# A two-layer hybrid decoder trunk: the last two weight sums of a feed-forward unit made by adding transfers instead of VectorE adds

## The chip, the cores and the metric

The kernel runs on one core of a Trainium2 chip. The metric is the device time of one execution in microseconds (us). Before the change three runs took 1273.28 us in the median, from 1272.17 to 1274.06.

Names used below: PE is TensorE (matmuls), PEld its weight loads, DVE is VectorE, ACT is ScalarE, POOL is GpSimd, SP is SyncE, which issues most DMA transfers. SBUF is the on-chip memory, PSUM holds matmul results. Every engine works through its own queue in order.

## The reference, cut to what matters

Two layers over 528 positions (16 learned meta tokens and 512 real ones) of width 1024. Each layer has a normalised input projection into two groups of heads (forgetting attention and retention), an output projection, and a SwiGLU feed-forward network (FFN) of width 2816. The change is in the FFN alone:

```python
hn = rmsnorm(h, ffn_norm_g)
ff = jax.nn.silu(jnp.einsum('bld,df->blf', hn, w_gate)) * jnp.einsum('bld,df->blf', hn, w_up)
return h + jnp.einsum('blf,fd->bld', ff, w_down)
```

All of it is float32. The outputs are the 512 real positions after a last normalisation.

## The kernel before

Activations lie transposed, 128 features on the partitions and the positions along the free axis. A weight tile has 128 partitions and 8 blocks of 128 columns (NK = 8, HB = 4 is half of them). For float32 accuracy on PE each operand is split into a high part (a cast, made on ACT) and a low part (what is left, made on DVE, or on POOL in the attention stage), and each product is three matmuls: high by high, high by low, low by high.

The FFN of a layer has 22 column tiles f. The first three (PLAIN) are multiplied plainly: one product with w_gate and one with w_up for each, through `dense_steps` (matmuls at L217). The other 19 of each layer, 38 in all, are units of the class `Unit` (matmuls at L881). A unit computes the gate and the up product of one f together by Winograd's form of Strassen's scheme: the two operands are cut into 2 by 2 blocks, and seven half-size products are made where eight would be needed. For that it wants sums of weight blocks beside the weights. With a = w_gate (tile `raw`) and b = w_up (tile `fraw`), each in a first half [0:HB] and a second half [HB:NK], the sums are:

- s[HB:NK] = the second half of w_up plus its first half (tile `Sw`). SP loads the one half, POOL issues a transfer that adds the other half from DRAM into it (L908).
- b[0:HB] = the first half of w_up plus the first half of w_gate, by such an adding transfer too (L909).
- s[0:HB] = s[HB:NK] + a[0:HB], an add on DVE (L917), in `make2`.
- a[HB:NK] = a[HB:NK] + s[0:HB], an add on DVE (L928), in `make4`.

Each unit has four weight jobs, and each job is a "make" that splits its weights into high and low: make1 (w1, from raw), make2 (w2, from Sw), make3 (w3, from fraw), make4 (w4, from the second half of raw). The head of a unit multiplies with w1 (two products, the first into PSUM bank x, the second into z), the middle with w2 (x, then y) and w3 (x), the tail with w3 (x) and w4 (y). After each of the first three products into x, ACT copies the bank into `e` (L947). Between the middle and the tail, and after the tail, stands a piece of the down projection of an earlier round (L1016).

What sets the order: the program is written as a list of steps. PE's order is that of the list. For DVE, ACT, POOL and SP a scheduler orders the instructions by its own estimate of when each can run, and the waits come from who reads and writes a tile. Buffers set how far loads run ahead: three for `raw`, two each for `fraw` and `Sw`, two for each ring of split weights. `need` makes a job and up to two after it, and a unit's loads are issued when its first job is fetched.

At the start of an FFN three things run together: the plain products, with a pair of casts on ACT (L191) and subtractions on DVE (L194) for each weight tile; the normalisation's factors (L295 to L300, from sums of squares at L331 to L340); and the sums and differences of activations that the units need (L842 to L847, tiles `S`, `th`, `tl`), in which the constant `neg`, the negated FFN norm weights, is used. The loads for the first two units are issued there too.

Of the kernel before, what the change touches and what calls it, by code (L numbers as in the profile page):

```python
# [13 lines left out]
ALU = mybir.AluOpType  # L14

D = 1024
NK = D // 128
# [3 lines left out]
DEPTH = 2  # L21
# [7 lines left out]
HB = NK // 2  # L29
# [10 lines left out]
def hybrid_kernel(ctx, tc, x_t, w_in, w_fl, w_out, w_gate, w_up, w_down, vecs, b_fg, rope, decay, mask, ident, out_t):  # L40
    nc = tc.nc
# [13 lines left out]
    vec = const.tile([128, vecs.shape[1]], F32, name="vec")  # L55
# [214 lines left out]
    def at(tag, dt=F32R, shape=(128, T), bufs=None):  # L270
        return phase["att"].tile(list(shape), dt, name=tag, tag=tag, bufs=bufs)

    def fft(tag, dt=F32R, shape=(128, T), bufs=None):
        return phase["ffn"].tile(list(shape), dt, name=tag, tag=tag, bufs=bufs)
# [79 lines left out]
    V_ATTN, V_FFN, V_FIN, V_GN = 0, 2 * NK, 4 * NK, 5 * NK  # L354
# [439 lines left out]
    def ffn(l, st, real, last):  # L794
# [73 lines left out]
        def splits(hi, lo, src):  # L868
            nc.scalar.copy(hi, src)  # L869
            nc.vector.tensor_sub(lo, src, hi.bitcast(F32))  # L870
# [17 lines left out]
        class Unit:  # L888
# [12 lines left out]
            def load(self):  # L901
                if "a" not in self.t:
                    for n, src, pool, tag, bufs in (("a", w_gate, wp, "raw", 3), ("b", w_up, phase["ffn"], "fraw", 2)):
                        self.t[n] = pool.tile([128, NK, 128], F32, name=tag, tag=tag, bufs=bufs)
                        nc.sync.dma_start(self.t[n], src[l, self.f])
                    s = self.t["s"] = fft("Sw", F32, (128, NK, 128), 2)
                    nc.sync.dma_start(s[:, HB:NK], w_up[l, self.f][:, HB:NK])
                    nc.gpsimd.dma_start(s[:, HB:NK], w_up[l, self.f][:, 0:HB], accum_op=ALU.add)  # L908
                    nc.gpsimd.dma_start(self.t["b"][:, 0:HB], w_gate[l, self.f][:, 0:HB], accum_op=ALU.add)  # L909

            def make1(self, hi, lo):
                splits(hi, lo, self.t["a"])


            def make2(self, hi, lo):
                a, s = self.t["a"], self.t["s"]
                nc.vector.tensor_add(s[:, 0:HB], s[:, HB:NK], a[:, 0:HB])  # L917
                nc.scalar.activation(hi, s, AF.Copy, scale=-1.0)
                nc.vector.scalar_tensor_tensor(lo, s, -1.0, hi.bitcast(F32), ALU.mult, ALU.subtract)

# [3 lines left out]


            def make4(self, hi, lo):
                a, s = self.t["a"], self.t["s"]
                nc.vector.tensor_add(a[:, HB:NK], a[:, HB:NK], s[:, 0:HB])  # L928
                splits(hi, lo, a[:, HB:NK])

            def bank(self, n):
                def go():
# [53 lines left out]
        def down_job(p, f0, f1):  # L986

            n = f1 - f0
            t = {}

            def load():
                if t:
                    return
                t["r"] = wp.tile([128, NK, 128], F32, name="raw", tag="raw", bufs=3)
                for s in range(2):
                    nc.sync.dma_start(t["r"][:, s * n:s * n + n], w_down[l, 2 * p + s, :, f0:f1])

            return add_job(load=load, make=lambda hi, lo: splits(hi, lo, t["r"][:, 0:2 * n]), n=2 * n)
# [223 lines left out]
        return steps  # L1222

    neg = const.tile([128, DEPTH * HB], F32, name="neg")
    for i in range(DEPTH):
        nc.vector.tensor_scalar_mul(neg[:, HB * i:HB * i + HB], vec[:, V_FFN + NK * i + HB:V_FFN + NK * i + NK], -1.0)
    gf = const.tile([128, NK], F32, name="gf")
    nc.vector.tensor_scalar_mul(gf, vec[:, V_FIN:V_FIN + NK], RSC)

    def layer(l):  # L1230
# [5 lines left out]
        ret = [{} for _ in range(RH)]  # L1236

        def ropes():
            for i, n in enumerate(("cr", "sr")):
                t = at(n, F32)  # L1240
                nc.sync.dma_start(t, rope[i])
                nc.vector.scalar_tensor_tensor(t, t, RSC, ly["R"], ALU.mult, ALU.mult)
                ly[n] = t
# [66 lines left out]
        for g in range(2):  # L1310
# [15 lines left out]
                      ret_places(3, 52, 45.5, 47.5, 57.5, 55.5, 58.5, 60, 64.1, 63, 64.2))  # L1326
        plan += [op[3], op[7], op[11], op[15]] + op[16:]
        up = ffn(l, ff, real, real)
        plan += [lambda: enter("ffn"), start_ffn] + up
        return plan  # L1330
# [78 lines left out]
```

## Time and profile before

| | |
|---|---|
| median of 3 runs | 1273.28 us |
| profiled execution, its own time | 1271.45 us |
| its span | 1269.6 us |
| PE, DVE, ACT, POOL busy | 99%, 75%, 54%, 26% of the span |
| clock granted to PE | 0.998 |
| first unit's head in layer 0 and in layer 1 | at 323.36 and 946.15 us |

A row of a timeline is: start, length, engine, line, operation, written tile <- read tiles, shapes, and in brackets how long the engine stood before it and what ended that. A row of a group of instructions is: line, engine, operation, count | busy us in total, mean ns of one | idle before, with what ended it. A row of DMA issues is: what is written <- what is read, the queue that issued it, the count, the size of one, and the median us from issue to landing. A queue named q1 carries the transfers that SP issues, q0 those of POOL.

### The profile page before, as it was taken

The page shows a single profiled execution, that of the slowest core. Times are in us where ns is not written, and L with a number is a line of the kernel's source. Part 1 is how long each engine was busy: PE and PEld are TensorE (multiplying, and loading weights), DVE is VectorE, ACT ScalarE, POOL GpSimd, SP SyncE. Part 2 cuts the span into 40 slices and gives each one's busy share as a digit, 9 for nine tenths or more (in the row PEclk, how much of TensorE's full clock was granted, in tenths as well). Part 3 has the DMA queues.
Part 4 walks back from the last instruction along what each step waited for, and adds up shares of the span by engine and source line. Part 5 has one row for each costly group of instructions (what it writes and reads, how often), then busy time and mean ns, then how long its engine had stood idle before and what let it go on. Part 6 is the DMA issues. An engine that isn't in the chain of part 4 may idle for free.

```text
span 1269.6 us, 23847 instructions
## 1 busy us (share of the span) xinstructions
PE 1254.7 (99%) x9271; PEld 1196.5 (94%) x9271; DVE 952.7 (75%) x1769; ACT 687.7 (54%) x1246; POOL 330.2 (26%) x598
## 2 busy tenths in 40 slices
PE   9999999999999999999999999999999999999997
PEld 8999999999999999999999989998789999999996
DVE  8877756779777777777786877467897777777766
ACT  7666545676444444444456665557764444444444
POOL 3355546421111111110025545554201111111100
PEclk9999999999999999999999999999999999999999
DMA  6322222226555555553323232222456655555521
GB/s 218 93 75 84 87 85 77 66 68 165 155 147 150 150 150 150 150 150 108 101 77 118 67 99 78 84 84 67 128 140 164 158 150 150 151 156 151 148 77 67
DMA packets 62098, 150.48 MB, mean 119 GB/s; under 512 B 7184, under 2 KB 14096, under 8 KB 61984
## 3 DMA queue, kind: packets, MB, share of 16 engines
q1 hardware_dynamic: 50576, 128.70, 30.5%
q0 software_dynamic: 10944, 19.93, 10.5%
q8 instruction: 73, 1.20, 0.4%
q10 hardware_dynamic: 464, 0.32, 0.1%
q14 instruction: 41, 0.34, 0.1%
HBM read 146.79 MB, written 2.13 MB: 117 GB/s over the span
## 4 chain that ended last, share of the span: by engine, by line
PE 93%; DVE 3%; ACT 2%; DMA 1%; issue 1%; DVEq 0%; ACTq 0%; SPq 0%
PE psd L217 29%; PE psa L881 19%; PE psd L1016 14%; PE psd L881 13%; PE psa L217 5%; PE psa L1016 4%; PE psa L418 2%; PE psa L573 2%; PE psa L507 2%; PE psa L730 1%; PE psa L700 1%; DVE ss L340 0%; DMA h<-x_t 0%; ACT whi L191 0%; PE psa L290 0%
## 5 line engine op out<-in xcount | busy, mean ns | idle before, releaser
L194 POOL TENSOR_TENSOR wlo<-raw,whi 128x128 fp32r<-128x128 f32 x504 | 259.0, 548 | 287.9 <-ACT whi L191 287.8
L217 PE MATMUL psd<-xh,whi 128*128 128x264 f32 (+1 forms) x792 | 195.8, 315 | 0.5 <-ACT whi L191 0.5
L217 PE MATMUL psd<-xl,whi 128*128 128x264 f32 (+1 forms) x792 | 186.1, 302 | 0.5 <-DVE xl L320 0.4
L217 PE MATMUL psd<-xh,wlo 128*128 128x264 f32 (+1 forms) x792 | 186.5, 303 | 0.0
L217 PEld LDWEIGHTS psd<-xh,whi 128*128 128x128 f32 x792 | 128.3, 189 | 5.5 <-ACT whi L191 1.2
L217 PEld LDWEIGHTS psd<-xh,wlo 128*128 128x128 f32 x792 | 126.8, 188 | 6.3 <-DVE wlo L194 0.4
L217 PEld LDWEIGHTS psd<-xl,whi 128*128 128x128 f32 x792 | 127.5, 189 | 5.0 <-DVE xl L320 1.2
L191 ACT CAST whi<-raw 128x512 fp32r<-128x512 f32 (+1 forms) x168 | 98.3, 613 | 49.7 <-PE psd L217 37.4
L908 POOL DMA_DIRECT2D Sw<-w_up x38 | 33.7, 888 | 324.7 <-DVE h L1023 248.7
L870 DVE TENSOR_TENSOR fwlo<-raw,fwhi 128x1024 fp32r<-128x1024 f32 (+2 forms) x62 | 64.0, 1032 | 36.3 <-ACT fwhi L869 36.1
L909 POOL DMA_DIRECT2D fraw<-w_gate x38 | 33.2, 874 | 220.2 <-DMA fraw<-w_up 145.4
L870 DVE TENSOR_TENSOR wlo<-raw,whi 128x1024 fp32r<-128x1024 f32 (+2 forms) x62 | 62.9, 1015 | 35.0 <-ACT whi L869 34.8
L869 ACT CAST whi<-raw 128x1024 fp32r<-128x1024 f32 (+2 forms) x62 | 54.9, 885 | 50.3 <-PE psd L881 38.6
L869 ACT CAST fwhi<-raw 128x1024 fp32r<-128x1024 f32 (+2 forms) x62 | 55.6, 897 | 47.2 <-PE psd L881 39.6
L881 PE MATMUL psa<-th,whi 128*128 128x264 f32 (+1 forms) x232 | 65.4, 282 | 0.0
L881 PE MATMUL psa<-th,wlo 128*128 128x264 f32 (+1 forms) x232 | 65.4, 282 | 0.0
L881 PE MATMUL psa<-tl,whi 128*128 128x264 f32 (+1 forms) x232 | 65.3, 282 | 0.0
L881 PE MATMUL psa<-th,fwhi 128*128 128x264 f32 (+1 forms) x224 | 63.4, 283 | 0.0
L881 PE MATMUL psa<-tl,fwhi 128*128 128x264 f32 (+1 forms) x224 | 63.3, 283 | 0.0
L881 PE MATMUL psa<-th,fwlo 128*128 128x264 f32 (+1 forms) x224 | 63.2, 282 | 0.0
L527 ACT ACTIVATE probs<-probs,nmax 128x144 f32<-128x144 f32 (+1 forms) x64 | 36.9, 576 | 44.2 <-DVE nmax L514 31.3
L947 ACT COPY e<-psa 128x264 f32<-128x264 f32 (+1 forms) x114 | 42.8, 375 | 28.0 <-PE psa L881 23.9
(341 smaller groups left out, 3980.1 us busy)
## 6 DMA issues: line engine op xcount, KB each, us to landing
raw<-w_in SPq DMA_DIRECT2D x54, 512.0 KB, 3.5
raw<-w_gate SPq DMA_DIRECT2D x44, 512.0 KB, 4.1
fraw<-w_up SPq DMA_DIRECT2D x38, 512.0 KB, 4.8
raw<-w_down SPq DMA_DIRECT2D x64, 256.0 KB, 2.9
Sw<-w_up SPq DMA_DIRECT2D x38, 256.0 KB, 2.6
fraw<-w_gate POOLq DMA_DIRECT2D x38, 256.0 KB, 4.1
Sw<-w_up POOLq DMA_DIRECT2D x38, 256.0 KB, 4.6
raw<-w_out SPq DMA_DIRECT2D x16, 512.0 KB, 3.5
```

Source lines behind the costliest of these rows:

```text
L191: pin(nc.scalar.copy(hi, job["raw"][:, c0:c1]), pinned)
L194: pin(sub(lo[:, i:i + step], job["raw"][:, c0 + i:c0 + i + step], hi[:, i:i + step].bitcast(F32)), pinned)
L217: nc.tensor.matmul(ps[1][b][:, 0:c1 - c0], w[:, wk, :], x[:, c0:c1], start=(k == 0 and i == 0), stop=(k == n - 1 and i == 2))
L418: nc.tensor.transpose(ps[:, 128 * j:128 * j + 128], src[:, o:o + 128], idt)
L527: nc.scalar.activation(pr, pr, AF.Exp, bias=nmax[0:nq], scale=-1.0, accum_out=rsum)
L869: nc.scalar.copy(hi, src)
L870: nc.vector.tensor_sub(lo, src, hi.bitcast(F32))
L881: nc.tensor.matmul(bank()[:, 0:b.shape[-1]], a[:, o + k, :], b, start=(fresh and k == 0 and i == 0), stop=(k == n - 1 and i == 2), skip_gr ...
L908: nc.gpsimd.dma_start(s[:, HB:NK], w_up[l, self.f][:, 0:HB], accum_op=ALU.add)
L909: nc.gpsimd.dma_start(self.t["b"][:, 0:HB], w_gate[l, self.f][:, 0:HB], accum_op=ALU.add)
L947: nc.scalar.copy(self.t["e"][:, i], self.t["x"][:, 0:w])
L1016: nc.tensor.matmul(v[:, 0:c1 - c0], a[:, s * n + k, :], b[:, c0:c1], start=(k == 0 and i == 0), stop=(k == n - 1 and i == 2))
```

## The change

Both DVE adds go. In `load`, SP also loads the first half of w_gate into s[0:HB], and POOL issues a third transfer, which adds s[HB:NK] to it, from SBUF into SBUF. In `make2`, POOL issues a fourth, which adds s[0:HB] into a[HB:NK], also within SBUF; make4 only splits. The values are the same sums. Each of the 38 units so has one more load of 256 KB on SP's queue, two more adding transfers of 256 KB on POOL's, and two adds of 128x512 fewer on DVE. The constant `neg`, which was computed for both layers at the program's start, is now computed in each layer, in `ropes`.

```diff
                     s = self.t["s"] = fft("Sw", F32, (128, NK, 128), 2)
                     nc.sync.dma_start(s[:, HB:NK], w_up[l, self.f][:, HB:NK])
+                    nc.sync.dma_start(s[:, 0:HB], w_gate[l, self.f][:, 0:HB])
                     nc.gpsimd.dma_start(s[:, HB:NK], w_up[l, self.f][:, 0:HB], accum_op=ALU.add)
                     nc.gpsimd.dma_start(self.t["b"][:, 0:HB], w_gate[l, self.f][:, 0:HB], accum_op=ALU.add)
+                    nc.gpsimd.dma_start(s[:, 0:HB], s[:, HB:NK], accum_op=ALU.add)
...
             def make2(self, hi, lo):
                 a, s = self.t["a"], self.t["s"]
-                nc.vector.tensor_add(s[:, 0:HB], s[:, HB:NK], a[:, 0:HB])
+                nc.gpsimd.dma_start(a[:, HB:NK], s[:, 0:HB], accum_op=ALU.add)
                 nc.scalar.activation(hi, s, AF.Copy, scale=-1.0)
                 nc.vector.scalar_tensor_tensor(lo, s, -1.0, hi.bitcast(F32), ALU.mult, ALU.subtract)
...
             def make4(self, hi, lo):
-                a, s = self.t["a"], self.t["s"]
-                nc.vector.tensor_add(a[:, HB:NK], a[:, HB:NK], s[:, 0:HB])
-                splits(hi, lo, a[:, HB:NK])
+                splits(hi, lo, self.t["a"][:, HB:NK])
...
     neg = const.tile([128, DEPTH * HB], F32, name="neg")
-    for i in range(DEPTH):
-        nc.vector.tensor_scalar_mul(neg[:, HB * i:HB * i + HB], vec[:, V_FFN + NK * i + HB:V_FFN + NK * i + NK], -1.0)
...
         def ropes():
+            nc.vector.tensor_scalar_mul(neg[:, HB * l:HB * l + HB], vec[:, V_FFN + NK * l + HB:V_FFN + NK * l + NK], -1.0)
```

In the changed kernel the lines from L908 to make2 are numbered one or two higher (L908 and L909 are L909 and L910, L918 and L919 are L920 and L921); L911 and L919 are the new transfers, and behind `make4` the numbers are the old ones again, up to neg. PE's order is the same instruction by instruction. On the other engines the scheduler places what follows anew. Three places matter for what follows, all at the start of layer 1's FFN. First ACT, from the last step of the normalisation's factor R on; the numbers behind the names of semaphores in brackets only say which one is waited for (DMAHW for a transfer of SP, DMASW for one of POOL). Before:

```order
L296 ACTIVATE R<-R 128x512 [waits Activation_49]
L142 CAST th_11870<-S 128x1024 [waits DVE_49]
L191 CAST whi<-raw 128x512 [waits DMAHW2_49,PE_49]
L191 CAST whi<-raw 128x512
L842 ACTIVATE S<-h_75,vec 128x512 [waits DVE_49]
L842 ACTIVATE S<-h_76,vec 128x512 [waits DVE_49,Activation_49]
L191 CAST whi<-raw 128x512 [waits DMAHW7_49,PE_49]
L407 ACT_TABLE_LOAD
L407 ACTIVATE sg<-sg 128x512 [waits DVE_49]
```

With the change:

```order
L296 ACTIVATE R<-R 128x512 [waits Activation_49]
L920 ACTIVATE fwhi<-Sw 128x1024 [waits DMASW7_49,DMASW5_49]
L191 CAST whi<-raw 128x512 [waits DMAHW5_49,PE_49]
L142 CAST th_11889<-S 128x1024 [waits DVE_49]
L191 CAST whi<-raw 128x512
L842 ACTIVATE S<-h_75,vec 128x512 [waits DVE_49]
L842 ACTIVATE S<-h_76,vec 128x512 [waits DVE_49]
L191 CAST whi<-raw 128x512 [waits DMAHW4_49,PE_49]
L407 ACT_TABLE_LOAD
L407 ACTIVATE sg<-sg 128x512 [waits DVE_49]
```

The cast of the first unit's Sw (L918 before, 17 rows further down, behind the last `th`) now stands directly behind R, ahead of the casts of the second plain product, and waits for two of POOL's transfers. In layer 0 the same cast has moved up in the same way, to between the two rows `S<-h_75` and `S<-h_76` of L842.

Second POOL, from its first transfer in this FFN on (the two units' transfers; `Sw<-Sw` and `raw<-Sw` are the new ones). Before:

```order
L909 DMA fraw<-w_gate 128x512 [waits DMAHW2_49,DMAHW3_49,DMASW5_49,DVE_49]
L908 DMA Sw<-w_up 128x512 [waits DMASW4_49,DMAHW4_49,DMASW3_49,DVE_49]
L909 DMA fraw<-w_gate 128x512 [waits DMAHW5_49]
L908 DMA Sw<-w_up 128x512 [waits DMAHW6_49,DMASW2_49]
L908 DMA Sw<-w_up 128x512 [waits DMASW7_49,DMAHW7_49,DVE_49,Activation_49]
```

With the change:

```order
L910 DMA fraw<-w_gate 128x512 [waits DMAHW5_49,DMAHW6_49,DMASW1_49,DVE_49]
L909 DMA Sw<-w_up 128x512 [waits DMASW5_49,DMAHW7_49,DMASW3_49,DVE_49]
L910 DMA fraw<-w_gate 128x512 [waits DMAHW1_49]
L911 DMA Sw<-Sw 128x512 [waits DMAHW0_49,DMASW5_49]
L909 DMA Sw<-w_up 128x512 [waits DMAHW2_49,DMASW2_49]
L911 DMA Sw<-Sw 128x512 [waits DMAHW3_49,DMASW0_49]
L919 DMA raw<-Sw 128x512 [waits DMAHW5_49,DMASW7_49,DMAHW6_49,DVE_49,Pool_49]
```

The first unit's `Sw<-Sw` stands third behind its `Sw<-w_up`, for whose landing it waits (DMASW5), with the second unit's fraw between them. The order in layer 0 is the same.

Third DVE, at the end of the same stretch, ahead of the first unit. Before:

```order
L194 TENSOR_TENSOR wlo<-raw,whi 128x512
L917 TENSOR_TENSOR Sw<-Sw,raw 128x512 [waits DMAHW1_49,DMASW7_49]
L143 TENSOR_TENSOR tl_11873<-S,th_11872 128x1024 [waits Activation_49]
L817 SCALAR_TENSOR_TENSOR sg<-psd,R 128x512 [waits PE_49]
L870 TENSOR_TENSOR wlo<-raw,whi 128x1024 [waits Activation_49]
L919 SCALAR_TENSOR_TENSOR fwlo<-Sw,fwhi 128x1024 [waits Activation_49]
```

With the change:

```order
L143 TENSOR_TENSOR al_12011<-tq,ah_12010 128x512 [waits Activation_49]
L921 SCALAR_TENSOR_TENSOR fwlo<-Sw,fwhi 128x1024 [waits DMASW7_49,DMASW5_49]
L143 TENSOR_TENSOR tl_11892<-S,th_11891 128x1024 [waits Activation_49]
L817 SCALAR_TENSOR_TENSOR sg<-psd,R 128x512 [waits PE_49]
L870 TENSOR_TENSOR wlo<-raw,whi 128x1024 [waits DMAHW6_49,Activation_49]
```

The add L917 is gone, and the low part of w2 (`fwlo<-Sw`), which stood behind that of w1 (`wlo<-raw`, 128x1024), now stands ahead of it.

## The prediction

> **What bounds the kernel now.** I read the busy table of the page first, then who TensorE (PE) waits for, then the chain of waits around the start of an FFN, then the busy time of a few stretches. From the page, and from the waits of PE over the whole span (who waits for whom: us in total, times, longest; nine rows in all, the first and the last two shown):
>
> ```profile
> PE 1254.7 (99%) x9271; PEld 1196.5 (94%) x9271; DVE 952.7 (75%) x1769; ACT 687.7 (54%) x1246; POOL 330.2 (26%) x598
> PE psa L1261 <- DVE wide L61: 1.6, 1, 1.6
> ...
> PE psd L217 <- DVE xl L320: 0.4, 1, 0.4
> PE psa L418 <- DVE psa L513: 0.2, 1, 0.2
> ```
>
> PE is busy for 1254.7 of 1269.6 us, and its nine waits come to 6.6 us in the whole program. None of them has L881 or L1016, the lines of the units and of the down projections. So a faster VectorE (DVE) has nothing to give in the units: what the change can do to the time is almost only to make PE wait where it does not wait now.
>
> The next rows are the chain of waits at the start of layer 1's FFN (start, length, what), then the busy time of four stretches (stretch, length, then the engines; the last three figures are clock, DMA share and GB/s; the last two rows are of DVE alone):
>
> ```profile
> 929.56 16.59 PE psd L217 x72
> 946.15 1.43 PE psa L881 x12
> ...
> 421.05:437.10 16.05, 16.05 (x135) 16.05 (x134) 11.74 (x18) 7.17 (x10) 1.71 (x2) 1.00 0.56 148
> 912.00:931.00 19.00, 18.62 (x80) 14.49 (x79) 18.49 (x33) 11.81 (x19) 3.50 (x4) 1.00 0.88 240
> 306.00:323.36 17.36, 17.04 (x28) 1.00 0.28 85
> 929.56:946.15 16.59, 16.37 (x27) 1.00 0.29 88
> ```
>
> Two kinds of stretch follow from this. In a unit in the middle of a layer (421.05 to 437.10) DVE works 11.74 us of 16.05 and the DMA engines 56%: there is room. At the start of an FFN, where the three plain products run and everything for the first unit is prepared, DVE has 0.2 to 0.3 us free in some 17 us, and just before it the DMA engines are 88% busy. A delay put into DVE there is not made up before the first unit.
>
> **The change part by part.** *What leaves DVE.* The two adds of a unit, and what an added transfer of this form costs today (groups of instructions; then a tile's landing times; then the two queues in the unit from 421.05, as packets, MB and share of the 16 engines):
>
> ```profile
> L917 DVE TENSOR_TENSOR Sw<-Sw,raw 128x512 f32<-128x512 f32 x38 | 26.1, 687 | 6.9 <-DMA raw<-w_gate 4.9 <-DMA Sw<-w_up 1.8
> L928 DVE TENSOR_TENSOR raw<-raw,Sw 128x512 f32<-128x512 f32 x38 | 25.9, 681 | 0.0
> DMA to landing us min/median/max: 4.1/4.6/11.8
> q1 hardware_dynamic: 720, 1.82, 32.3%
> q0 software_dynamic: 288, 0.52, 23.4%
> ```
>
> 52 us of DVE go. By the waits above that is worth nothing in the units; I put the gain at 0, its bounds at 0 and 0.5 us (the 0.4 us wait of PE for a DVE row at L217, rounded up). A loss from the removal itself is excluded, since no instruction is added to DVE.
>
> *What comes in the steady units.* Each unit gets one plain load of 256 KB and two added transfers of 256 KB. From the q1 row, 0.323 x 16.05 / 1.82 MB = 2.85 us of all engines per MB, so 0.75 us for the load. From the q0 row, 0.234 x 16.05 / 2 = 1.88 us for an added transfer that reads DRAM. One that reads SBUF does not occur in this trace; from below I bound it by the plain load, 0.75, from above by twice 1.88, and take 1.88, the row that shares the adding. Then 0.56 x 16.05 + 0.75 + 2 x 1.88 = 13.5 of 16.05 us: busier, but not full. The landing times also fit, by two rows of the unit at 421 and the row of neg at the program's start (DVE and ACT by time):
>
> ```profile
> 3.90 0.24 DVE L1226 TENSOR_SCALAR neg<-vec 128x4 f32<-128x4 f32 x2 [0.95 <-DMA vec<-vecs]
> 420.65 1.22 DVE L870 TENSOR_TENSOR fwlo<-raw,fwhi 128x1024 fp32r<-128x1024 f32 x1 [1.90 <-ACT fwhi L869]
> 432.71 0.62 ACT L869 CAST fwhi<-raw 128x512 fp32r<-128x512 f32 x1 [1.01 <-PE psd L881]
> ```
>
> The add into raw can go out when the first split of the unit has read raw, at 420.65 + 1.22 = 421.87, and lands 4.1 to 4.6 us later, about 426.5; its reader, make4's cast, comes at 432.71. Six us of cover hide it. If that cover were gone, the cast would hold ACT's queue, and behind it the copy of e (L947), for which PE waits before its next product into the same bank: each us late is a us of PE. The add of Sw has more room still, since with two Sw buffers a unit's Sw is loaded and summed one unit before its cast. POOL, which is busy 1.71 of 16.05 us, has room for two more issues. So 0 for the steady units.
>
> *The constant neg.* Four columns of 128 are moved a few places in DVE's queue; the two of them take 0.24 us together, after a wait for `vec` that the next row of DVE has as well. I put it at 0, bounds 0.2 either way.
>
> *The start of the FFN, layer 1.* Here the change moves work. ACT's cast of the first unit's Sw (L918, now L920) stands right after L296, where before it came 17 rows later, and it waits for the second added transfer, Sw into Sw. That one waits for the first to land. The rows: POOL's issues; landing times (us from issue) of the first Sw, the second fraw and the second Sw; ACT and DVE by time.
>
> ```profile
> 917.15 0.98 POOL L908 DMA_DIRECT2D Sw<-w_up  x1
> 919.15 0.86 POOL L909 DMA_DIRECT2D fraw<-w_gate  x1 [1.02 <-DMA fraw<-w_up]
> 920.04 0.87 POOL L908 DMA_DIRECT2D Sw<-w_up  x1
> Sw<-w_up POOLq DMA_DIRECT2D x1, 256.0 KB, 7.1
> fraw<-w_gate POOLq DMA_DIRECT2D x1, 256.0 KB, 7.7
> Sw<-w_up POOLq DMA_DIRECT2D x1, 256.0 KB, 8.8
> 922.84 0.63 ACT L296 ACTIVATE R<-R 128x512 f32<-128x512 f32 x1
> 924.32 1.14 ACT L191 CAST whi<-raw 128x512 fp32r<-128x512 f32 x2
> 924.96 0.69 DVE L194 TENSOR_TENSOR wlo<-raw,whi 128x512 fp32r<-128x512 f32 x1
> 942.56 1.22 DVE L870 TENSOR_TENSOR wlo<-raw,whi 128x1024 fp32r<-128x1024 f32 x1
> 943.69 1.22 DVE L919 SCALAR_TENSOR_TENSOR fwlo<-Sw,fwhi 128x1024 fp32r<-128x1024 f32 x1
> ```
>
> The first Sw lands at 917.15 + 7.1 = 924.25, so the new transfer goes out at 924.3. Ahead of it in POOL's queue is the second fraw, which landed at 926.85; its own load now has 256 KB more before it on SP (0.75 us), so 927.6. The transfer behind that fraw landed 2.0 us after it (928.84 against 926.85): 929.6. Bounds: 924.3 + 4.1 = 928.4 below; above, behind fraw at half the engines' rate (2 x 1.88) and at twice the price (1.88 more), 933. I take 929.6, since the second Sw is the nearest row in size, place and load.
>
> ACT is at this cast at 923.47 and now stands until 929.6. The cast takes 1.06 us, the next, whi of the second plain product, 0.6, so DVE starts its wlo at 931.3 instead of 924.96: 6.3 us late. DVE has 0.2 us free until 946.15, so this delay reaches the first unit's wlo (L870, ending at 943.78). It gains 0.60 us by the L917 row that is gone and loses 1.13 us because fwlo<-Sw now stands ahead of it: it ends at 943.78 + 6.3 - 0.6 + 1.1 = 950.6. PE wants it with the third matmul of the unit's head, 946.15 + 0.24 = 946.4. PE stands for 4.2 us in the products before and at the head. (The second plain product itself asks at 929.56 + 0.46 for what is ready at 932.0; those 2.0 us are part of the 4.2.) Then the add into raw goes out at 950.7, lands at 955.3 by the median of 4.6, the cast and the copy of e after it (about 1 us) end at 956.3, while PE, four products of 1.43 us after the head's start and 4.2 late, is at that bank at 956.1: 0.2 us more, 0.3 with the issue. Layer 1: **4.5 us**, with bounds of 3.3 and 7.9 from the two landings.
>
> *The start of the FFN, layer 0.* The same cast is moved between the two scalings S of L842, with the same queue on POOL. POOL's issues of the second fraw and the second Sw, their landing times, and ACT and DVE by time:
>
> ```profile
> 294.26 1.04 POOL L909 DMA_DIRECT2D fraw<-w_gate  x1
> 294.89 1.30 POOL L908 DMA_DIRECT2D Sw<-w_up  x1
> fraw<-w_gate POOLq DMA_DIRECT2D x1, 256.0 KB, 10.6
> Sw<-w_up POOLq DMA_DIRECT2D x1, 256.0 KB, 11.8
> 301.47 1.41 ACT L842 ACTIVATE S<-h,vec 128x528 f32<-128x528 f32 x2
> 307.25 0.70 DVE L826 TENSOR_TENSOR tq<-tq,sg 128x528 f32<-128x528 f32 x1
> 319.75 1.22 DVE L870 TENSOR_TENSOR wlo<-raw,whi 128x1024 fp32r<-128x1024 f32 x1
> ```
>
> The second fraw landed at 304.9, with the load 305.6; the next 1.8 later: 307.4 (bounds 1.2 below and 3.4 above, as in layer 1). After it ACT has the cast (1.06), S (0.7), a table load (1.28) and sg (0.65) to do, so sg is there at about 310.9, and DVE's tq<-tq,sg, at 307.25 before, is 3.7 us late. At the unit: 319.75 + 1.22 + 3.7 - 0.6 = 324.1 against PE's 323.36 + 0.24 = 323.6: **0.5 us**, bounds 0 and 3.9.
>
> *Sum.* 0 + 0 + 0 + 4.5 + 0.5 = 5.0 us, bounds 3.3 and 11.8. The profiled execution took 1271.45 us around its span of 1269.6, 1.8 us under the median of the runs, 1273.28; so about 1276.4 for a profiled execution and **1278** for the median, this case's own range being 1276.6 to 1285.1.
>
> The landing time is the term that decides. [...]
>
> **The rivals.** *The sum lands in time.* A transfer that reads SBUF may land like a plain load of its size, and not queue behind fraw:
>
> ```profile
> Sw<-w_up SPq DMA_DIRECT2D x38, 256.0 KB, 2.6
> ```
>
> Then it lands at 924.3 + 2.6 = 926.9, ACT is free 2.7 us earlier than I said, layer 1 costs 4.2 - 2.7 = 1.5 and layer 0 nothing: 1274.8. It decides from a landing at 927.6 downwards. For it: the HBM queue is not read. Against it: fraw ahead in the same queue, 88% busy engines, and no added transfer under 4.1 us.
>
> *The DMA engines become the bound.* If adding from SBUF costs twice 1.88 us, a unit needs 9.0 + 0.75 + 7.5 = 17.3 us of transfers in 16.05: 1.2 us for each of 38 units, about 47 us, 1320. It decides from 3.15 us per transfer. Nothing in the trace speaks for the double price; only that such a transfer is not in it.
>
> *Faster.* DVE's 52 us shorten a wait of PE. The place would have to be among the nine waits, which no L917 or L928 row stands before in an FFN; it needs 2.5 of their 6.6 us. Price 0.5 us at the most by the row at L217.
>
> **How the numbers follow.** 0.2% is 2.5 us, about what a measurement of this kernel can tell from no change. Late start 0.64 (1276.6 to 1285.1, all slower); sum in time 0.24 (same); DMA bound 0.07 (slower); faster 0.05. So slower 0.71, same 0.24, faster 0.05. The time is the late start's, 1278. The range goes down to 1273.5, to hold the sum in time, and up to 1286, a little over the upper bound of the sum; the DMA-bound and the faster case, 0.12 together, are left out, and with the edges about 0.2.
>
> **What would show it.** In the changed profile: PE waits at L217 and L881 after 924 for a DVE or ACT row, some 4 us in layer 1 and under 1 in layer 0, and before them ACT idle at L920, released by the transfer into Sw, landing near 929.6 and 307.4. The steady units keep 16.05 us with a DMA share near 0.84, and DVE falls by about 52 us. The forecast is wrong if ACT does not stand at that cast (then the first rival), if the units grow (the second), or if DVE takes the delay up before 946.

## The result, and the profile after

The changed kernel takes **1378.85 us** (median of 4 runs, 1371.8 to 1381.88), the kernel before 1272.72 us (median of 4, 1272.08 to 1274.06): a ratio of 1.0828, 95% interval 1.0805 to 1.0851. The prediction was slower, by 5 us; it is slower by 106. Its range, 1273.5 to 1286, is left far behind.

The profiled execution took 1371.8 us, its span is 1370.0, 100.4 us more than before. First the busy table, and the first rows of who PE waits for (us in total, times, longest):

```profile
PE 1284.9 (94%) x9271; PEld 1218.9 (89%) x9271; DVE 908.2 (66%) x1693; ACT 678.4 (50%) x1246; POOL 397.0 (29%) x674
```

```profile
PE psa L881 <- ACT e L947: 64.8, 31, 5.1
PE psd L217 <- DVE sg L817: 5.7, 1, 5.7
```

The first row of waits did not exist before. It belongs to the units: PE wants to start the next product into a bank, and ACT has not yet copied the last one out of it (e, L947). With the start of layer 1's FFN (the second row) that is 70.5 us, and PE's idle time has grown by as much: 1370.0 - 1284.9 = 85.1 us against 1269.6 - 1254.7 = 14.9, that is 70.2 more. The other 30.2 us are in PE's busy time itself, 1284.9 against 1254.7, for the same 9271 matmuls. The last section comes back to them.

Why is ACT late? Its two new waits over the whole span, and its rows in one unit (start, length, operation, in brackets the idle time before it and what ended it):

```profile
ACT fwhi L869 <- DMA raw<-Sw: 79.0, 18, 7.6
ACT whi L869 <- DMA raw<-Sw: 65.9, 17, 5.9
```

```profile
439.38 0.62 ACT L869 CAST whi<-raw 128x512 fp32r<-128x512 f32 x1 [4.48 <-DMA raw<-Sw]
439.91 0.63 ACT L142 CAST ah<-tq 128x528 fp32r<-128x528 f32 x1
440.44 0.37 ACT L947 COPY e<-psa 128x264 f32<-128x264 f32 x1
```

The cast of the unit's fourth weight sum stands for 4.48 us until the new transfer into raw has landed, and the copy of e stands behind it. This is what the prediction named as the price "if that cover were gone". The cover was six us; where did it go? POOL's issues of the same stretch show it:

```profile
424.20 0.87 POOL L909 DMA_DIRECT2D Sw<-w_up  x1 [7.34 <-DMA Sw<-w_up]
432.20 0.86 POOL L911 DMA_DIRECT2D Sw<-Sw  x1 [7.14 <-DMA Sw<-w_up]
432.75 1.21 POOL L910 DMA_DIRECT2D fraw<-w_gate  x1
433.28 1.58 POOL L919 DMA_DIRECT2D raw<-Sw  x1
443.35 0.88 POOL L909 DMA_DIRECT2D Sw<-w_up  x1 [8.48 <-DVE fwlo L870]
451.42 0.86 POOL L911 DMA_DIRECT2D Sw<-Sw  x1 [7.20 <-DMA Sw<-w_up]
451.96 1.22 POOL L910 DMA_DIRECT2D fraw<-w_gate  x1
452.50 1.57 POOL L919 DMA_DIRECT2D raw<-Sw  x1
```

The row to see is 432.20. POOL has stood there for 7.14 us, because the second add of a Sw may only be issued when the first has landed. And behind it in the same queue stands raw<-Sw, which belongs to **the unit before** and needs nothing of all that. It goes out at 433.28 and 452.50, 19.22 us apart. The chain of waits over the same stretch and a little further (start, length, what) closes it:

```profile
433.28 6.00 DMA raw<-Sw
...
452.50 5.87 DMA raw<-Sw
...
458.43 2.64 DMA Sw<-w_up
...
461.64 0.17 POOL Sw L909
461.81 7.77 issue
469.58 0.04 POOLq L910
469.62 0.54 POOL Sw L911
```

The landing of raw<-Sw sets a Sw buffer free, since it is now the last that reads it (there are two). Only then can SP load the next Sw into it (2.64 us); only then can POOL issue the first add (0.6 us later); it lands some 7.8 us after that; only then come the second add, fraw, and the next raw<-Sw, 0.5 us apart each, which lands 5.9 us later. That is **a ring of waits**, one unit long, through a buffer, SP, POOL and the DMA engines. By these rows it takes 5.9 + 2.6 + 0.6 + 7.8 + 1.1 = 18.0 us, while PE needs 16.05 us for a unit of layer 0. So the ring sets the unit. Over all 36 intervals between two adds into raw of the same layer the median is 18.0 us; in the kernel before, the median from one cast of Sw to the next is 16.0 us in layer 0 and 15.5 in layer 1. (The profile puts POOL's wait ahead of the first add down to the load of Sw in 25 of the 38 units. The wait at 443.35 is put down to a row of DVE instead, so this one turn is not shown to go by the load.)

Before, POOL had two transfers in a unit:

```profile
430.81 0.86 POOL L908 DMA_DIRECT2D Sw<-w_up  x1 [8.91 <-DVE h L1023]
437.30 0.86 POOL L909 DMA_DIRECT2D fraw<-w_gate  x1 [5.62 <-DMA fraw<-w_up]
```

It waited for the landing of a load then too (5.62 us), but nothing that stood behind this wait was the last reader of a Sw buffer: that was DVE's add L928. So this ring was not closed. The busy times of two units of the changed kernel (stretch, length, then PE, PEld, DVE, ACT, POOL, and at the end clock, DMA share and GB/s) show what it does to the engines:

```profile
421.00:440.00 19.00, 16.28 (x132) 16.07 (x132) 10.56 (x15) 7.46 (x12) 3.53 (x4) 1.00 0.66 166
440.00:459.00 19.00, 17.82 (x132) 17.61 (x132) 10.56 (x15) 6.76 (x11) 3.52 (x4) 0.91 0.68 167
```

No engine is full, and the DMA engines (the last figure but one) are at 0.66 to 0.68. A full resource is not what bounds this kernel; a chain that comes round is.

### The profile page after: what moved, and what is told of

It reads as the page before. It is cut to its first block, busy times and chain, and to the rows that moved or that the text cites. A ratio compares the mean times of both kernels' runs of the same rounds, so it can differ in the third digit from the quotient of the medians.

```text
span 1370.0 us, 24036 instructions
## 1 busy us (share of the span) xinstructions
PE 1284.9 (94%) x9271; PEld 1218.9 (89%) x9271; DVE 908.2 (66%) x1693; ACT 678.4 (50%) x1246; POOL 397.0 (29%) x674
## 3 DMA queue, kind: packets, MB, share of 16 engines
q0 software_dynamic: 21888, 39.86, 17.4%
## 4 chain that ended last, share of the span: by engine, by line
PE 50%; DMA 20%; issue 19%; DVE 4%; POOL 3%; ACT 3%; POOLq 0%; SPq 0%; ACTq 0%; DVEq 0%
PE psd L217 27%; DMA raw<-Sw 13%; DMA Sw<-w_up 5%; PE psa L881 4%; PE psd L1016 4%; PE psa L217 4%; PE psa L418 2%; PE psd L881 2%; PE psa L573 2%; PE psa L507 1%; POOL Sw L911 1%; PE psa L730 1%; POOL fraw L910 1%; PE psa L700 1%; PE psa L1016 1%
## 5 line engine op out<-in xcount | busy, mean ns | idle before, releaser
L194 POOL TENSOR_TENSOR wlo<-raw,whi 128x128 fp32r<-128x128 f32 x504 | 258.1, 546 | 290.2 <-ACT whi L191 290.0
L870 DVE TENSOR_TENSOR fwlo<-raw,fwhi 128x1024 fp32r<-128x1024 f32 (+2 forms) x62 | 64.1, 1033 | 73.7 <-ACT fwhi L869 73.7
L909 POOL DMA_DIRECT2D Sw<-w_up x38 | 34.1, 896 | 261.4 <-DMA Sw<-w_up 188.9
L870 DVE TENSOR_TENSOR wlo<-raw,whi 128x1024 fp32r<-128x1024 f32 (+2 forms) x62 | 63.0, 1016 | 63.9 <-ACT whi L869 63.8
L911 POOL DMA_DIRECT2D Sw<-Sw x38 | 32.7, 861 | 247.0 <-DMA Sw<-w_up 247.0
L881 PE MATMUL psa<-th,fwhi 128*128 128x264 f32 (+1 forms) x224 | 67.8, 303 | 36.3 <-ACT e L947 36.3
L881 PE MATMUL psa<-th,whi 128*128 128x264 f32 (+1 forms) x232 | 68.9, 297 | 28.4 <-ACT e L947 28.4
L881 PEld LDWEIGHTS psa<-th,fwhi 128*128 128x128 f32 x224 | 44.5, 199 | 40.1 <-ACT e L947 39.6
L1023 DVE TENSOR_TENSOR h<-psd,h 128x512 f32<-128x512 f32 (+1 forms) x69 | 47.9, 694 | 38.7 <-PE psd L1016 38.7
L881 PEld LDWEIGHTS psa<-th,whi 128*128 128x128 f32 x232 | 45.1, 194 | 31.9 <-ACT e L947 31.5
L919 POOL DMA_DIRECT2D raw<-Sw x38 | 55.7, 1465 | 54.1 <-DVE wlo L870 54.1
```

The lines of the kernel that those rows point to most:

```text
L194: pin(sub(lo[:, i:i + step], job["raw"][:, c0 + i:c0 + i + step], hi[:, i:i + step].bitcast(F32)), pinned)
L881: nc.tensor.matmul(bank()[:, 0:b.shape[-1]], a[:, o + k, :], b, start=(fresh and k == 0 and i == 0), stop=(k == n - 1 and i == 2), skip_gr ...
L911: nc.gpsimd.dma_start(s[:, 0:HB], s[:, HB:NK], accum_op=ALU.add)
L919: nc.gpsimd.dma_start(a[:, HB:NK], s[:, 0:HB], accum_op=ALU.add)
L1023: nc.vector.tensor_add(sv(h[m], real), pv(ps[0], real), sv(h[m], real))
```

## The experiments

Three theories went into the first runs. *Loop*: the ring just described. *Traffic*: the added transfers cost by themselves, 106 us for the three of a unit. *Buffers*: two Sw buffers are too few. All ratios are to the kernel before, run on the same chip, with 95% intervals.

**The inner sum alone.** The add into raw goes back to DVE, the two transfers into Sw stay.

```diff
 def make2:
-    nc.gpsimd.dma_start(a[:, HB:NK], s[:, 0:HB], accum_op=ALU.add)
 def make4:
+    nc.vector.tensor_add(a[:, HB:NK], a[:, HB:NK], s[:, 0:HB])
```

> Only the sum inside Sw is made by transfers; the add into raw stays on DVE. Three theories. Loop: in the changed kernel the unit's length is set by a ring of waits: the add into raw lands, which frees a Sw buffer; the next Sw loads (2.6 us); its first add lands (about 8 us in the burst); POOL, which issues in order, has waited for that, and only then issues the add into raw, which lands 5.9 us later: 17.7 to 19 us per unit. Without the add into raw there is no ring, so units of 16.05 us, and only the start of layer 1's FFN is left: 1273 to 1279 us. Traffic: the new transfers cost by themselves, so two of the three new ones leave about two thirds of the 106 us: about 1343. Start only: 1279 or less as well, so this run doesn't tell it from the loop.

Measured: 1279.71 us against 1272.21, ratio 1.0066 (1.0049 to 1.0083). Its units run at PE's pace, in 250 us of layer 1 without a gap; the loss is one wait at the start of layer 1's FFN. A stretch of its units, PE's longest wait, ACT's rows ahead of it, and the clock behind it (last figure but two):

```profile
1000.00:1250.00 250.00, 250.00 (x1730) 232.53 (x1729) 174.87 (x245) 114.62 (x161) 36.22 (x42) 1.00 0.67 169
```

```profile
922.52 0.63 ACT L296 ACTIVATE R<-R 128x512 f32<-128x512 f32 x1
928.81 1.06 ACT L919 ACTIVATE fwhi<-Sw 128x1024 fp32r<-128x1024 f32 x1 [5.66 <-DMA Sw<-Sw]
930.40 0.69 DVE L194 TENSOR_TENSOR wlo<-raw,whi 128x512 fp32r<-128x512 f32 x1 [5.82 <-ACT whi L191]
934.78 0.76 PE L217 MATMUL psd<-xh,whi 128*128 128x512 f32 x1 [5.55 <-DVE sg L817]
```

```profile
934.80:938.20 3.40, 3.40 (x8) 2.72 (x9) 3.40 (x8) 2.00 (x4) 0.00 (x0) 0.50 0.42 154
```

This is the predicted chain at the start of layer 1, to within a microsecond: ACT was to stand until 929.6 and stands until 928.81, DVE's wlo was to come at 931.3 and comes at 930.40. What follows is larger than predicted: 5.55 us of PE instead of 4.2, and then half the clock (0.50) in the 3.40 us behind it. (The wait stands before the fourth of the six plain products, the one with w_up of the second column tile.)

**The add into raw alone.** The inner sum goes back to DVE.

```diff
 def load:
-    nc.sync.dma_start(s[:, 0:HB], w_gate[l, self.f][:, 0:HB])
-    nc.gpsimd.dma_start(s[:, 0:HB], s[:, HB:NK], accum_op=ALU.add)
 def make2:
+    nc.vector.tensor_add(s[:, 0:HB], s[:, HB:NK], a[:, 0:HB])
     nc.gpsimd.dma_start(a[:, HB:NK], s[:, 0:HB], accum_op=ALU.add)
```

> Only the add into raw is a transfer; the sum inside Sw stays on DVE. Loop: POOL no longer has to wait for a landing between the first add of the next Sw and the add into raw. The ring is then 2.6 (load) + about 1.1 (two issues) + 5.9 (landing) = 9.6 us, under the unit's 16.05 us, so it doesn't bind: 1271 to 1277 us. Traffic: one of three new transfers, about 1308. A theory by which the landing time of the add into raw alone makes ACT late (5.9 us against the cover that I had reckoned) would see ACT wait at the fourth cast here too and give over 1300.

Measured: 1272.19 against 1272.21 us, ratio 0.9999 (0.999 to 1.0009). The part that makes ACT late in the changed kernel costs nothing on its own. So the two parts cost 7.5 and 0 us apart, and 106 together: the loss is in their combination, which neither traffic (a sum of prices) nor a late landing by itself can give.

**A third Sw buffer.**

```diff
-    s = self.t["s"] = fft("Sw", F32, (128, NK, 128), 2)
+    s = self.t["s"] = fft("Sw", F32, (128, NK, 128), 3)
```

> The whole change with three Sw buffers in place of two (a small tile of the attention is moved to another pool to make room). Loop: the order of POOL puts the add into raw of unit X behind the adds of unit X+2's Sw now, and these wait for the buffer that the add into raw of X-1 frees, so the ring is closed as before and has the same length: 1365 to 1385 us. Buffers: if the shortage of Sw buffers alone were the cause, a third gives each load a unit more, and the time falls to 1273 to 1285. Traffic: 1379.

Measured: 1379.85 us, ratio 1.0854 (1.0836 to 1.0873), no gain. The scheduler uses the third buffer to place the loads and adds of Sw one unit further ahead in the queues, and the ring closes as before: raw<-Sw of a unit now stands behind the adds of the unit after the next. The median interval between two adds into raw is 18.1 us here, 18.0 in the changed kernel. The theory of too few buffers falls.

**The first add of Sw behind the add into raw.** All transfers are the same; one is kept in the order in which the program names it.

```diff
-    nc.gpsimd.dma_start(s[:, HB:NK], w_up[l, self.f][:, 0:HB], accum_op=ALU.add)
+    pin(nc.gpsimd.dma_start(s[:, HB:NK], w_up[l, self.f][:, 0:HB], accum_op=ALU.add))
```

> The whole change, with the first add of a unit's Sw pinned in POOL's queue behind the add into raw of the unit before; nothing else changes, and all transfers are the same. Loop: the ring is cut, since the add into raw can go out as soon as its data are there: units of 16.05 us, ACT without waits at the fourth cast, 1274 to 1282 us (the start of layer 1's FFN keeps its 4 to 6 us). Traffic: 1379. Buffers: about 1379, since the two buffers are the same.

Measured: 1300.62 us, ratio 1.0230 (1.0198 to 1.0263). The order of one queue gives back 78 us of 106, with the same traffic; but 1274 to 1282 was expected, and that is missed. Two waits of ACT, and the one of PE at L947, show what I had overlooked:

```profile
ACT whi L920 <- DMA Sw<-Sw: 48.0, 9, 7.1
ACT fwhi L920 <- DMA Sw<-Sw: 46.8, 9, 6.9
```

```profile
PE psa L881 <- ACT e L947: 4.8, 8, 1.0
```

The ring is cut (the 64.8 us at L947 have shrunk to 4.8), but now both adds of a Sw start only after the add into raw of the unit before, and the second lands too late for its own reader, the cast of Sw (L920): ACT stands there 18 times for about 5 us. PE meets this mostly one step later: DVE's sg (L957) stands in its queue behind the low part of the late Sw, and PE waits for it four times, 6.1 us in all. Another 5.8 us are the start of layer 1, and PE's busy time is 10.3 us longer (1265.0 against 1254.7). The order solves one unit's problem at the cost of the next one's.

**The second add alone behind the add into raw.** The first keeps its early place.

```diff
+    with tc.issue_after(summed[0].ins) if summed else ExitStack():
         nc.gpsimd.dma_start(s[:, 0:HB], s[:, HB:NK], accum_op=ALU.add)
```

(`summed` holds the add into raw that make2 issued last.)

> The whole change, all transfers the same, but the second add of a unit's Sw is put in POOL's queue behind the add into raw of the unit before; the first add keeps its early place. So POOL waits for no landing between the landing of a Sw load and the add into raw, and the sum of Sw is not started a whole unit later, as it was in the run with the first add pinned (there ACT waited 18 times about 5 us for the second add). Loop: the ring is 2.6 + 1.1 + 5.9 = 9.6 us, so units of 16.05 us; the start of layer 1's FFN keeps its cost of the run with the sum of Sw alone, 7.5 us: 1276 to 1283 us. If the adding transfers are too late anyway in this amount, whatever their order: 1295 or more.

Measured: 1280.68 against 1271.98 us, ratio 1.0074 (1.0056 to 1.0091), as expected: the units are back at PE's pace, and what is left, 8.7 us, is about the 7.5 us of the inner sum alone.

**The same, and the first unit's inner sum on DVE.** In the first unit of each layer the load and the second add are left out and DVE adds as before.

```diff
+    if self.f > PLAIN:
         nc.sync.dma_start(s[:, 0:HB], w_gate[l, self.f][:, 0:HB])
...
+    if self.f == PLAIN:
+        nc.vector.tensor_add(s[:, 0:HB], s[:, HB:NK], a[:, 0:HB])
```

> The kernel with the second add behind the add into raw, and in the first unit of each layer the inner sum of Sw made by DVE as before (no load and no second add for that unit). Loop with the start: if the 7.5 us of the start come from ACT's cast of the first Sw, which waits for its second add while it stands at the head of ACT's queue, they go: 1271 to 1276 us. If the start is late for another reason (the DMA engines' load ahead of it), 1277 to 1283.

Measured: 1272.21 against 1271.98 us, ratio 1.0000 (0.9991 to 1.0009). The whole 106 us are gone, with 36 of 38 inner sums and all 38 adds into raw still made by transfers. (The run also takes a load and a transfer out of each start, so by itself it does not part ACT's wait from their traffic; ACT's row in the run with the inner sum alone, 5.66 us of standing, does.) Its busy table and a stretch of its units:

```profile
PE 1254.3 (99%) x9271; PEld 1196.6 (94%) x9271; DVE 908.2 (72%) x1695; ACT 687.9 (54%) x1246; POOL 396.3 (31%) x672
```

```profile
421.00:440.00 19.00, 19.00 (x158) 19.00 (x157) 11.84 (x18) 7.42 (x11) 6.00 (x7) 1.00 0.80 201
```

DVE has 44.5 us less to do than before (908.2 against 952.7), and PE's busy time is what it was: the repaired change is worth what the prediction gave for DVE's adds, nothing. One number that I had written down is wrong here: the ring of this order was to take 9.6 us. Over a whole layer POOL issues the add into raw at about PE's pace, which says nothing of the ring; but where it catches up in layer 0, from 423.94 to 438.06, the interval is still 14.1 us. POOL reaches this add only behind the one into fraw, which waits for the load of fraw (4.41 us at 437.53). This wait does no harm, since no cast of a unit's weights waits for a transfer in this run; but the room in the ring is less than I thought.

**The traffic alone.** The kernel before, with the three transfers of a unit going to and from tiles that nobody reads, in 34 of 38 units (DVE's adds stay; a small tile of the attention is moved to make room, as in the run with three buffers).

```diff
+    if self.f > PLAIN + 1:
+        nc.sync.dma_start(spare[0].rearrange("p (a b) -> p a b", a=HB), w_gate[l, self.f][:, 0:HB])
+        for i in (1, 0):
+            pin(nc.gpsimd.dma_start(spare[i], st["x"][i][1][:, META:T].bitcast(F32), accum_op=ALU.add))
```

> The kernel before, with DVE's adds as they were, and beside them in all but the first two units of a layer the change's three transfers of 256 KB with nobody waiting for them: a load from w_gate into a spare tile, and two adding transfers from SBUF into spare tiles, issued by POOL behind the unit's own adds. Traffic: 34 of 38 units carry the load, so 34/38 of 106 us: about 1367. Loop: the transfers cost nothing by themselves, and POOL's two issues take no one's place: 1271 to 1277 us.

Measured: 1276.56 against 1271.98 us, ratio 1.0042 (1.0025 to 1.0059): 4.6 us, not 95. A stretch of it:

```profile
421.00:440.00 19.00, 19.00 (x159) 19.00 (x158) 13.91 (x20) 7.85 (x12) 6.07 (x7) 1.00 0.84 206
```

The DMA engines are busier here (0.84) than in the changed kernel (0.66), and PE has no gap in this stretch. Of the 4.6 us, 2.5 are four waits of PE for DVE's h (L1032) in the down projections. Traffic falls as the cause of the 106 us.

**The constant alone**, on the kernel before:

> The kernel before with the constant neg computed at its new place and nothing else. Every theory: 1272 to 1273 us; a difference of more than 2 us would mean that the move of the constant is a part of the loss that no theory has.

Measured: 1272.15 against 1271.98 us, ratio 1.0000 (0.9991 to 1.0009).

**The ring made longer, and shorter.** If a ring sets the unit, its length can be set. For the longer one the changed kernel gets one more adding transfer that nobody needs, which makes POOL wait for the landing of the second add as well:

```diff
     nc.gpsimd.dma_start(s[:, 0:HB], s[:, HB:NK], accum_op=ALU.add)
+    if self.f > PLAIN + 1:
+        pin(nc.gpsimd.dma_start(spare[0], s[:, 0:HB], accum_op=ALU.add))
     nc.gpsimd.dma_start(self.t["b"][:, 0:HB], w_gate[l, self.f][:, 0:HB], accum_op=ALU.add)
```

> The changed kernel with one more adding transfer in all but the first two units of a layer: from the sum in Sw into a spare tile, in POOL's queue between the second add of Sw and the add of fraw. Nobody waits for what it writes, but it reads what the second add writes, so POOL holds until that has landed (3.3 us) and spends 0.5 us on one more issue, before the add into raw may go. Loop: the ring grows by 3.8 to 4.4 us in 34 units: 1380 + 130 to 150, 1500 to 1535 us. Traffic: one transfer of 256 KB more, by the run with three spare transfers 0 to 2 us: 1378 to 1385.

For the shorter one the add into fraw is moved from just ahead of the add into raw to just behind it:

```diff
+    with tc.issue_after(summed[0].ins) if summed else ExitStack():
         nc.gpsimd.dma_start(self.t["b"][:, 0:HB], w_gate[l, self.f][:, 0:HB], accum_op=ALU.add)
```

> The changed kernel with the add into fraw moved in POOL's queue from just ahead of the add into raw to just behind it; POOL still waits for the landing of the first add of Sw ahead of both. Loop: the ring stays closed, but loses one issue (0.5 us) and, since the add into raw then has one transfer less ahead of it, some of its 5.9 us of landing (down to about 4.5): 0.5 to 1.9 us less in some 36 units, so 1310 to 1360 us. Traffic: no change, 1379. If a single position in the queue were all that matters (the add into raw directly behind the one that it waits for), it would fall to 1280.

Measured: 1492.38 us, ratio 1.1724 (1.1701 to 1.1747), and 1320.65 us, ratio 1.0379 (1.0362 to 1.0395). POOL's issues of the longer one, then of the shorter one:

```profile
425.55 1.52 POOL L926 DMA_DIRECT2D raw<-Sw  x1
434.90 0.87 POOL L911 DMA_DIRECT2D Sw<-w_up  x1 [7.83 <-DMA Sw<-w_up]
442.63 0.86 POOL L915 DMA_DIRECT2D Sw<-Sw  x1 [6.86 <-DMA Sw<-w_up]
446.23 0.86 POOL L917 DMA_DIRECT2D spa<-Sw  x1 [2.74 <-DMA Sw<-Sw]
446.77 1.22 POOL L918 DMA_DIRECT2D fraw<-w_gate  x1
447.31 1.57 POOL L926 DMA_DIRECT2D raw<-Sw  x1
```

```profile
420.36 1.21 POOL L922 DMA_DIRECT2D raw<-Sw  x1
...
437.54 1.22 POOL L922 DMA_DIRECT2D raw<-Sw  x1
```

From one add into raw to the next: 21.76 us in the longer, 17.18 in the shorter; in the changed kernel the two intervals around there are 17.99 and 19.22. The medians of all 36 are 21.8, 16.4 and 18.0. So the longer ring is 3.7 us longer, just under the expected 3.8 to 4.4, and the shorter one 1.6 shorter, within 0.5 to 1.9. The longer kernel's total of 1492 misses the expected 1500 to 1535 by 8 us. The spans of the two profiled executions, 1494.5 and 1370.0, are 124.5 us apart, about 34 times 3.7. A transfer whose result nobody reads cost 113 us here when it stood in the ring, and three of them cost 4.6 us when they didn't. With that I take the ring as shown.

## Why the prediction was wrong, point by point

**The step that failed is the steady units, "So 0 for the steady units".** Within it, one sentence: "The add into raw can go out when the first split of the unit has read raw, at 420.65 + 1.22 = 421.87". That is when its data are ready. It is issued when POOL reaches it, and ahead of it POOL stands for the landing of another unit's first add. What I checked of POOL was its busy time ("has room for two more issues"); what decided was that the second add makes POOL wait, 247.0 us over the 38 units, 6.5 in the mean and 8.2 at most, and what is queued behind that wait. In place of the six us of cover the runs show a ring of 18.0 us against the 16.05 us of a unit. For ACT I named what stands behind the waiting cast; for POOL, in the steady units, I did not. The rows that would have shown it were before me, in POOL's order at the start of layer 1: `Sw<-w_up`, `Sw<-Sw`, and behind them the other unit's `raw<-Sw`.

The second half of the miss is that I took each transfer by itself, with a landing time and a reader, and never followed the release of its buffer. "A unit's Sw is loaded and summed one unit before its cast" is true, and it is just what puts the next unit's adds ahead of this unit's add into raw, while the buffer for those adds is set free by an add into raw. A delay in a chain is paid once; in a ring it is paid in every unit.

Two things in this step held. The price of a late cast, "each us late is a us of PE", was named rightly, with the place (L947); and the DMA engines do have the room that I gave them (0.80 busy in the stretch of the repaired kernel's units). The added transfers are even cheaper than the 1.88 us taken, by the software queue's row of the changed kernel (packets, MB, share of the 16 engines):

```profile
q0 software_dynamic: 21888, 39.86, 17.4%
```

17.4% of 1370.0 us are 238.4 us for 152 transfers, 1.57 us each.

**The start of layer 1: right as far as DVE's delay, too small behind it.** Predicted 4.5 us, measured 7.5 by the run with the inner sum alone (8.0 between the profiled spans, 1277.6 and 1269.6). The landing (928.81 against 929.6) and DVE's delay (5.4 us against 6.3) were even a little shorter than forecast. Two things were missed. PE does not lose the time at the unit's head, where I looked for most of it, but before the fourth of the six plain products (the prediction calls it the second), at 934.78, where it needs a PSUM bank that sg (L817) has still to read; the 2.0 us that I had seen in the products are 5.55. And the matmuls after that wait run at half the clock (0.50) in the 3.40 us that follow, which is 1.7 us that the sum had no term for. In the changed kernel, after the same wait (5.71 us, up to 981.54), PE is busy at half the clock for 5.87 us, up to 987.41.

**The start of layer 0: within its bounds of 0 and 3.9.** 0.5 us was predicted; neither the changed kernel nor the run with the inner sum alone shows a wait of PE there, and the run with the second add behind the add into raw has one of 0.3 us, for the row that was named (wlo, L870).

**DVE's adds and the constant: right.** 44.5 us left DVE and no time came out of it (ratio 1.0000 in the repaired kernel); the move of neg is 1.0000 as well. DVE's 952.7 falls to 908.2, not by the 52 us of the two groups: over 76 instructions that is 0.1 us each, about what a DVE row's length exceeds the distance to the next row's start (in the kernel before, L194 at 924.96 lasts 0.69 us, and the next starts 0.61 us later).

**The rivals.** The sum in time is out: in the run with the inner sum alone the first transfer from Sw into Sw is issued at 924.42 and the cast that waits for it starts at 928.81, 4.39 us later, where that rival needed at most 3.3. One reading against it was too strong: the kernel before has added transfers that land before 4.1 us, since those into fraw go down to 3.7. The faster kernel is out as well. "The DMA engines become the bound" named the right place, units that grow, and even a sizeable time (1320), but with the wrong mechanism: the run with the traffic alone is at 1276.56. By my own last sentence the forecast is "wrong if the units grow (the second)"; they grew, and it was not the second. What I had no rival for was a wait inside an in-order queue, the one resource whose busy time looked emptiest.

## What to carry to other kernels

An engine that issues transfers in order and waits for their landings is not judged by its busy time (POOL here: 29% busy, and 247.0 us of standing at one line): for each instruction in it that waits, list what stands behind it, whose work that is, and whether anything behind it sets free what the waiting one needs. If the list comes back to its start, add up the ring and compare it with the stage's period; a shorter one cost nothing here (the repaired kernel, ratio 1.0000), a longer one set the period (16.4, 18.0 and 21.8 us against 16.05 and less), and a third buffer did not help (18.1 us), since the scheduler used it to run further ahead. Two changes that each leave the units at their pace can make such a ring together, so a costing part by part has to be followed by one of the parts in their queue.

## What the runs showed of the hardware that I had not expected

**After 12 of PE's 27 waits of more than 1 us in the two FFNs the matmuls ran at a lower clock.** Most of the 30.2 us that PE's busy time grew are a lower granted clock behind some of the waits. PE's rows at the end of two waits in the changed kernel, and the 3.4 us after each (last figure but two: the clock):

```profile
440.86 0.39 PE L881 MATMUL psa<-th,whi 128*128 128x264 f32 x1 [2.03 <-ACT e L947]
569.26 0.39 PE L881 MATMUL psa<-th,fwhi 128*128 128x264 f32 x1 [2.07 <-ACT e L947]
```

```profile
440.86:444.26 3.40, 3.40 (x17) 3.40 (x18) 1.99 (x3) 1.28 (x2) 0.88 (x1) 0.56 0.91 278
569.26:572.66 3.40, 3.40 (x28) 3.40 (x29) 2.13 (x3) 1.27 (x2) 0.87 (x1) 1.00 0.97 313
```

Of the 27 waits, the 8 under 2 us are followed by the full clock; of the 14 between 2.03 and 2.94 us, 7 are followed by a lower one; all 5 from 3.52 us up are. Up to PE's last matmul the changed kernel's trace has twelve stretches at half the clock, ten of 3.41 us (one of them from 441.28 to 444.69, clock 0.50) and two of 6.83 (one from 980.58 to 987.41, clock 0.50); their starts lie whole multiples of 3.41 us apart. PE is busy for 44.75 us of them, so they account for 22.4 of the 30.2 us; where the other 7.8 come from stays open.

What parts two nearly equal gaps (2.03 and 2.07 us) in this trace shows when the span is cut into steps of 3.41 us, counted from the start of a slow stretch. The gap of 2.03 us ends at 440.86 and lies whole in the step from 437.86 to 441.28, in which PE is busy for only 1.39 us; the next step runs at half the clock (0.50). The gap of 2.07 us ends at 569.26 and is split by an edge at 567.57: PE is busy for 3.03 us in the step before the edge and for 1.72 in the one behind it, and the clock stays full (1.00). So it goes in the whole of the two FFNs: in each of the twelve steps ahead of a slow stretch PE stands for 1.90 us or more, and in every other step at full clock for 1.76 us at most. In this execution the two kinds of step are parted by how much of the step PE stands, and not by the length of one gap.

That the clock is lower because of the gaps, and not because of the transfers, rests on this and on the repaired kernel: nearly the same transfers, no wait of PE in its units, and PE's busy time of 1254.3. No run made gaps without anything else. So the changed kernel lost more than its waits: 30 us on top of 70, of which 22 are put down to the clock.

**In these runs the landing of an added transfer went more with what was issued ahead of it than with whether it reads SBUF or DRAM.** Landing times of the changed kernel by form (size of one, median us from issue to landing):

```profile
fraw<-w_gate POOLq DMA_DIRECT2D x38, 256.0 KB, 5.0
Sw<-w_up POOLq DMA_DIRECT2D x38, 256.0 KB, 7.4
Sw<-Sw POOLq DMA_DIRECT2D x38, 256.0 KB, 3.3
raw<-Sw POOLq DMA_DIRECT2D x38, 256.0 KB, 5.8
```

Sw<-Sw and raw<-Sw have the same size and kind. The first lands in 3.3 us and is issued when POOL has stood for the landing of the one ahead (7.14 us at 432.20); the last takes 5.8 and is issued directly behind two others, Sw<-Sw and fraw<-w_gate (0.54 us apart from 432.20 to 433.28). In the shorter ring, which swaps the last two, their figures swap too: raw<-Sw, now behind one, lands in 4.8 us, and fraw<-w_gate, from DRAM and now behind two, in 5.6. In the repaired kernel Sw<-Sw goes out directly behind raw<-Sw, and takes 5.5. Sw<-w_up took 4.6 us in the kernel before; in the ring, at 7.4, it goes out behind six loads that SP, released at one moment, issues in 2.3 us (439.74 to 442.02). But it takes 6.9 in the repaired kernel and with the traffic alone as well, where no ring binds, so the burst is not shown to be the reason.
